# A hybrid decoder block on one core: another order of seven products, denser block sums, a later second norm, and factors stored in two parts

## The chip, the cores and the metric

One core of a Trainium2 chip runs the whole block as one program. The metric is the time on the device in microseconds, from three runs of the kernel before: 2037.86, 2042.06 and 2042.62, median 2042.06. Everything is float32 in memory. Every product is made of three matmuls on reduced-precision (fp32r) operands: each operand is split into a high part, rounded by a copy on ScalarE, and a low part, the difference, made by VectorE; the kernel adds high x high, high x low and low x high.

## What is computed

Sequence 512, width 2048, feed-forward width 8192, depth one. In the reference, cut to what matters here:

```
h  = rmsnorm(x, norm_mix_g);  z = h @ w_in           # (512, 2048) x (2048, 5128)
merged = [rmsnorm(attention(z)), rmsnorm(spatial_gating(z))]
x  = x + merged @ w_out                              # 2048 x 2048
h2 = rmsnorm(x, norm_ffn_g)                          # the second norm
a  = relu(h2 @ w_ff1)                                # the first product, 2048 x 8192
x  = x + (a * a) @ w_ff2                             # the second product, 8192 x 2048
out = rmsnorm(x, norm_final_g)
```

rmsnorm divides each row by the root of the mean of its squares (plus 1e-6) and multiplies by a gain. The root of the second norm is a number per token, so it commutes with the first product; a squared ReLU takes it as a square. The kernel therefore multiplies by it only at the very end, when the second product's sums are added to x (`settle`, with the square of the inverse root in `r2`).

## The kernel before

**The projections.** `run_units` goes over 224 steps: ten units of 16 steps for the input projection, then four units `oa` (attention half of the output projection) and four `og` (spatial-gating half) of 8 steps. A step loads and splits a piece of weights and issues 12 matmuls of 512 columns; pieces are split three steps ahead (`AHEAD`). After a step's matmuls `tick` runs the other tasks: each is a generator that yields the number of steps until its next turn.

**The handover.** When a unit `og` c ends, `g_done(c)` (L606) adds the two halves and x into `oa[c]`, squares them on ScalarE, adds the squares up over k on GpSimd (`ffn["ss"]`), starts the transposes of the result (`turn_x2`, stored in DRAM as `x2d`), scales by the gain (`scale_x2`) and makes the left operands of the first product (`make_forms`). For c = 3 the first product's loads and first three splits are issued first. `norm2_task` (L651) then sums over partitions with one-column matmuls and takes the root into `r2`.

**The products by Strassen and Winograd.** Both feed-forward products run as seven products of half-size blocks, P1 to P7, where eight would be usual; operands are sums of blocks (forms A11, A12, A22, S1 to S4 on the left; blocks b11, b12, b21, b22 and their sums on the right). In the first product 16 blocks u have 4 parts j of 7 products: 448 groups of 12 matmuls with 256 columns. `prepare` splits a group's weights three groups ahead. Two of the seven (P6 and P4) need a further block added into a tile that is already on the chip; before, this add stands directly ahead of the split. After part 3 each product's sum is taken out of its PSUM bank (`evacuate`), squared, and combined.

**The block sums.** `sums_task` (L679) makes b11 + b12 and b22 + b12 for all 64 pairs (u, j): three loads, two adds on VectorE, two stores to DRAM (`t1d`, `t3d`), from where `load` of the first product reads them two parts ahead. It starts at step 18 of the projections. Its buffers are one deep. Its instructions are marked to keep their place in the program's order.

**The factors.** After a block u, `factors_task` (L815) forms the seven left operands of the second product from the squares, splits each into a tile of 128 x 2 x 512 (high and low), from the pool `raw_pool` of four buffers, which the loads of w1 use too, and stores it in DRAM (`fac`).

**What sets the order.** TensorE's instructions run in the order of the program. Those of the other engines are put in order by a planner, when the program is built, from estimated durations, with the program's order as priority; at run time each engine keeps that order, and waits where an operand or a buffer is not ready. In the first product a tick comes after every second group, in the second product after every group.

## Time and profile before

| what | us |
|---|---|
| median of three runs | 2042.06 |
| the profiled execution | 2042.68 |
| its span, first to last instruction | 2040.1 |
| projections, up to the first matmul of the first product | 696.3 |
| first product (L806) | 696.3 to 1394.8 |
| second product (L1069) and the end | from 1394.8 |
| busy: TensorE, VectorE, ScalarE, GpSimd | 1988.1, 1600.3, 1040.3, 105.7 |

PE is TensorE, PEld its loading of weights, DVE VectorE, ACT ScalarE, POOL GpSimd, SP the engine that issues the DMAs. A row of a matmul lasts from issue to the modelled end, so rows overlap and their busy time is a union; the number of matmuls in a stretch says more than the busy time. In lists of groups and waits `fh` and `fl` are the high and low halves of w1, `form` the left operands, `q` the banks of the first product, `wh` and `wl` the halves of w2, `fc` the factors' staging tile, `b` the block sums' tiles, `t` the tiles that hold b11 and the sums in the first product.

### The profile page before, as it was taken

Reading aid. Unit: us, or ns where it says so; the run is one execution under the profiler, and the core shown is the slowest. Engines: PE = TensorE matmul, PEld = TensorE weight load, DVE = VectorE, ACT = ScalarE, POOL = GpSimd, SP = SyncE. Lnnn points to the kernel's source line nnn. Section 1 sums busy time; section 2 is a strip of 40 time slices with the busy share of each in tenths; the row PEclk is TensorE's granted clock in tenths of the full one; section 3 lists DMA queues with packets and bytes.
Section 4 is the critical chain, followed back from the end, with each engine's and each line's share of the span. In section 5 each row is a group of like instructions: output and inputs, shape, how many; then the busy total and the mean of one; then the engine's idle time right before and its main releaser. Section 6 shows DMA issues by size and latency. Waiting matters only on the chain.

```text
span 2040.1 us, 30501 instructions
## 1 busy us (share of the span) xinstructions
PE 1988.1 (97%) x11296; PEld 1733.7 (85%) x11296; DVE 1600.3 (78%) x2399; ACT 1040.3 (51%) x1676; POOL 105.7 (5%) x99
## 2 busy tenths in 40 slices
PE   9999999999999889999999999999999999999997
PEld 6888888888887789999999999998888888888875
DVE  7467467676658868888888788889888898898897
ACT  6344344455326555565565566666444444444455
POOL 5000001000222200000000000000000000000000
PEclk9999999999999989999999999999999999999999
DMA  6455554567555568888886665668836636646632
GB/s 222 136 168 165 170 165 156 188 199 263 181 186 181 181 217 276 288 289 302 296 279 220 224 223 202 217 233 332 333 128 240 246 130 237 240 137 234 244 137 83
DMA packets 209892, 435.69 MB, mean 214 GB/s; under 512 B 17744, under 2 KB 95696, under 8 KB 209616
## 3 DMA queue, kind: packets, MB, share of 16 engines
q1 hardware_dynamic: 209056, 431.89, 62.0%
q8 instruction: 88, 1.44, 0.3%
q10 hardware_dynamic: 432, 1.35, 0.2%
q0 software_dynamic: 256, 0.52, 0.2%
q14 instruction: 60, 0.49, 0.1%
HBM read 333.03 MB, written 100.66 MB: 213 GB/s over the span
## 4 chain that ended last, share of the span: by engine, by line
PE 39%; DVE 13%; DMA 6%; issue 3%; ACT 2%; SPq 1%; POOLq 0%; POOL 0%; ACTq 0%; DVEq 0%
PE bX L1069 16%; PE q L806 12%; PE bZ L1069 7%; DVE fl L744 4%; PE bY L1069 4%; DMA fac<-fc 3%; DMA b<-in_w_dram 2%; DVE fc L822 1%; DVE wl L902 1%; DMA r<-in_w_dram 1%; ACT fh L743 1%; DVE t L740 1%; DVE b L687 0%; DVE b L686 0%; DVE acc L950 0%
## 5 line engine op out<-in xcount | busy, mean ns | idle before, releaser
L806 PE MATMUL q<-form,fh 128*128 128x256 f32 x3584 | 657.8, 285 | 9.8 <-ACT fh L743 6.6
L806 PEld LDWEIGHTS q<-form,fh 128*128 128x128 f32 x3584 | 565.1, 193 | 13.3 <-ACT fh L743 9.3
L806 PE MATMUL q<-form,fl 128*128 128x256 f32 x1792 | 515.3, 288 | 17.5 <-DVE fl L744 16.9
L806 PEld LDWEIGHTS q<-form,fl 128*128 128x128 f32 x1792 | 346.5, 193 | 26.7 <-DVE fl L744 25.5
L901 ACT CAST wh<-raw 128x1024 fp32r<-128x1024 f32 x224 | 234.3, 1053 | 225.4 <-PE bX L1069 120.7
L902 DVE TENSOR_TENSOR wl<-raw,wh 128x1024 fp32r<-128x1024 f32 x224 | 271.1, 1223 | 72.5 <-ACT wh L901 71.7
L1069 PE MATMUL bX<-wh,fac 128*128 128x512 f32 x1008 | 320.9, 392 | 1.8 <-ACT wh L901 1.6
L743 ACT CAST fh<-t 128x512 fp32r<-128x512 f32 x256 | 155.0, 617 | 155.2 <-DVE t L738 67.6
L1069 PEld LDWEIGHTS bX<-wh,fac 128*128 128x128 f32 x1008 | 189.2, 188 | 49.5 <-ACT k_wh L922 6.4
L744 DVE TENSOR_TENSOR fl<-t,fh 128x512 fp32r<-128x512 f32 x256 | 173.9, 689 | 66.5 <-ACT fh L743 66.4
L1069 PE MATMUL bX<-wl,fac 128*128 128x512 f32 x504 | 198.3, 393 | 3.3 <-DVE wl L902 3.3
L1069 PE MATMUL bZ<-wh,fac 128*128 128x512 f32 x512 | 162.8, 389 | 0.0
L1069 PEld LDWEIGHTS bX<-wl,fac 128*128 128x128 f32 x504 | 94.6, 188 | 27.2 <-DVE wl L902 9.0
L1069 PEld LDWEIGHTS bZ<-wh,fac 128*128 128x128 f32 x512 | 96.1, 188 | 19.9
L150 PE MATMUL ps_qk<-xh,wh_qk 128*128 128x512 f32 x256 | 101.7, 397 | 0.0
L152 PE MATMUL ps_qk<-xh,wl_qk 128*128 128x512 f32 x256 | 100.0, 391 | 0.0
L151 PE MATMUL ps_qk<-xl,wh_qk 128*128 128x512 f32 x256 | 99.8, 390 | 0.0
L1069 PE MATMUL bZ<-wl,fac 128*128 128x512 f32 x256 | 99.6, 389 | 0.0
L744 DVE TENSOR_TENSOR fl<-r,fh 128x512 fp32r<-128x512 f32 x128 | 88.0, 687 | 10.5 <-ACT fh L743 10.5
L163 DVE SCALAR_TENSOR_TENSOR wl_qk<-raw_qk,cols,wh_qk 128x512 fp32r<-128x512 f32 x64 | 47.8, 750 | 61.2 <-ACT wh_qk L162 58.8
L162 ACT ACTIVATE wh_qk<-raw_qk,cols 128x512 fp32r<-128x512 f32 x64 | 46.3, 723 | 93.9 <-PE ps_qk L151 59.2
L743 ACT CAST fh<-r 128x512 fp32r<-128x512 f32 x128 | 79.0, 617 | 22.0 <-PE q L806 19.4
(621 smaller groups left out, 3594.8 us busy)
## 6 DMA issues: line engine op xcount, KB each, us to landing
b<-in_w_dram SPq DMA_DIRECT2D x256, 256.0 KB, 4.3
raw<-in_w_dram SPq DMA_DIRECT2D x128, 512.0 KB, 4.9
fac<-fc SPq DMA_DIRECT2D x112, 512.0 KB, 3.5
fac<-fac SPq DMA_DIRECT2D x112, 512.0 KB, 6.0
r<-in_w_dram SPq DMA_DIRECT2D x64, 512.0 KB, 5.1
raw_qk<-in_win_dram SPq DMA_DIRECT2D x32, 512.0 KB, 3.8
t1d<-b SPq DMA_DIRECT2D x64, 256.0 KB, 3.3
t3d<-b SPq DMA_DIRECT2D x64, 256.0 KB, 3.3
```

The costliest lines, as they stand in the source:

```text
L150: nc.tensor.matmul(ps, lhsT=ah, rhs=bh, start=start, stop=False)
L151: nc.tensor.matmul(ps, lhsT=ah, rhs=bl, start=False, stop=False)
L152: nc.tensor.matmul(ps, lhsT=al, rhs=bh, start=False, stop=stop)
L162: nc.scalar.activation(wh, raw, AF.Copy, scale=g)
L163: nc.vector.scalar_tensor_tensor(wl, raw, g, f(wh), ALU.mult, ALU.subtract)
L740: nc.vector.tensor_tensor(b[P4], b[P4], b[P2], ALU.add)
L743: nc.scalar.copy(pairs(wh), b[p])
L744: nc.vector.tensor_tensor(pairs(wl), b[p], pairs(f(wh)), ALU.subtract)
L806: nc.tensor.matmul(d, lhsT=l[:, c], rhs=r, start=j == 0 and q == 0 and m == 0 and w == 0, stop=j == 3 and q == 1 and w == 2, skip_group_ch ...
L901: nc.scalar.copy(wh, s)
L902: nc.vector.tensor_tensor(wl, s, f(wh), ALU.subtract)
L1069: nc.tensor.matmul(banks[chain][t], lhsT=l, rhs=r, start=start and w == 0, stop=stop and w == 2, skip_group_check=True)
```

## The change

Four edits. (1) The second norm's squares, their sum and the small matmuls leave the handover; in the second product a new task `second_norm` reads x back from DRAM in eight loads of 512 KB, squares it on ScalarE with a running sum over the row, and forms `r2`; it starts in the middle of the second product and takes a turn every three groups. (2) A block sum takes four steps instead of five. (3) The first product takes its seven products in the order P5, P1, P6, P2, P7, P4, P3; the adds for P6 and P4 are made right after the splits of P5 and P6; the forms at the handover follow the new order, and transposes of c = 2 use other PSUM banks. (4) The factors' high parts go two to a staging tile, the low parts are written over the form itself, and both are stored on their own.

```
-                if k == 0:
-                    ffn["ss"] = const.tile([P, 512], F32, tag="ssum", name="ssf")
-                    nc.scalar.activation(ffn["ss"], o, AF.Square)
-                else:
-                    nc.scalar.activation(t, o, AF.Square)
-                    nc.gpsimd.tensor_tensor(ffn["ss"], ffn["ss"], t, ALU.add)
...
             elif c == 2:
-                make_forms(c, (A11, A12))
+                make_forms(c, (S1, A11))
             else:
-                make_forms(2, (S1, S2, S3, S4, A22))
-                make_forms(3, (A11, A12, S1, S2, S3, S4, A22))
-            if c == 3:
-                start_task(norm2_task(), 6)
+                make_forms(2, (S2, A12, S3, A22, S4))
+                make_forms(3, (S1, A11, S2, A12, S3, A22, S4))
...
-            pt = mm(f"px{c}_{m}") if c == 3 else ax(f"px{c}_{m}", m % 2)
+            pt = mm(f"px{c}_{m}") if c > 1 else ax(f"px{c}_{m}", m % 2)
...
+    first = (P5, P1, P6, P2, P7, P4, P3)
...
                 here(nc.sync.dma_start(out=t3d[u][j], in_=b22))
-                yield 2
+                yield 1
...
         def prepare(i):
-            if p == P6:
-                nc.vector.tensor_tensor(b[P6], b[P6], b[P3], ALU.add)
-            if p == P4:
-                nc.vector.tensor_tensor(b[P4], b[P4], b[P2], ALU.add)
...
             nc.vector.tensor_tensor(pairs(wl), b[p], pairs(f(wh)), ALU.subtract)
             ready[i] = wh, wl
-            if p == P4:
+            if p == P5:
+                nc.vector.tensor_tensor(b[P6], b[P6], b[P3], ALU.add)
+            if p == P6:
+                nc.vector.tensor_tensor(b[P4], b[P4], b[P2], ALU.add)
+            if p == P3:
                 load(*divmod(4 * u + j + 2, 4))
...
-        def put(i):
-            t = raw_pool.tile([P, 2, 512], F32R, tag="raw", name=f"fc{u}_{i}")
-            nc.scalar.copy(t[:, 0, :], form[i])
-            nc.vector.tensor_tensor(t[:, 1, :], form[i], f(t[:, 0, :]), ALU.subtract)
-            nc.sync.dma_start(out=fac[u][i], in_=f(t).rearrange("p a c -> p (a c)"))
...
+        for i in range(0, NF, 2):
+            n = min(2, NF - i)
+            yield 2
+            t = raw_pool.tile([P, 2, 512], F32R, tag="raw", name=f"fc{u}_{i}")
+            for k in range(n):
+                nc.scalar.copy(t[:, k, :], form[i + k])
+                nc.vector.tensor_tensor(form[i + k].bitcast(F32R), form[i + k], f(t[:, k, :]), ALU.subtract)
+                nc.sync.dma_start(out=fac[u][i + k][:, 512:1024], in_=form[i + k])
+            nc.sync.dma_start(out=fac[u][i:i + n, :, 0:512].rearrange("i p c -> p i c"), in_=f(t)[:, 0:n, :])
...
+        def second_norm():
+            for th in range(2):
+                for q in range(4):
+                    x2 = load_x2(th, q)
+                    for t in range(2):
+                        tb = 2 * th + t
+                        nc.scalar.activation(x2[:, t, :], x2[:, t, :], AF.Square, accum_out=sums[:, tb, q:q + 1])
+                    yield 3
+            nc.vector.tensor_reduce(r2, sums, axis=AX.X, op=ALU.add)
+            inv_root(r2, r2, D, NT)
+            nc.vector.tensor_tensor(r2, r2, r2, ALU.mult)
...
+            if (kc, n, p, h) == (NK // 2, 0, P1, 0):
+                start_task(second_norm())
```

## Rows read from the trace of the kernel before

**Rows 1.** Of the page, busy us (share) xinstructions; clock in tenths, forty slices.

```profile
PE 1988.1 (97%) x11296; PEld 1733.7 (85%) x11296; DVE 1600.3 (78%) x2399; ACT 1040.3 (51%) x1676; POOL 105.7 (5%) x99
...
PEclk9999999999999989999999999999999999999999
```

**Rows 2.** Windows of L806: length, PE and PEld busy (xinstructions), clock, DMA, GB/s.

```profile
696.30:759.50 63.20, 48.20 (x336) 45.74 (x337) 0.86 0.54 168
759.50:890.60 131.10, 126.41 (x1011) 123.40 (x1010) 0.99 0.85 290
890.60:1107.20 216.60, 208.34 (x1682) 203.12 (x1681) 1.00 0.81 279
1107.20:1394.80 287.60, 285.50 (x2354) 283.03 (x2352) 1.00 0.65 228
```

**Rows 3.** The waits of TensorE over the span: us in total, times, longest.

```profile
PE q L806 <- DVE fl L744: 16.9, 32, 3.5
...
PE ps_og L152 <- DVE wl_og L163: 2.9, 2, 1.9
```

**Rows 4.** Windows, all engines: PE, PEld, DVE, ACT, POOL, clock, DMA, GB/s.

```profile
635.00:640.00 5.00, 3.42 (x8) 2.75 (x9) 3.51 (x6) 0.07 (x1) 0.00 (x0) 0.66 0.72 226
...
696.20:722.50 26.30, 15.09 (x80) 13.43 (x80) 25.31 (x36) 15.19 (x28) 5.91 (x4) 0.74 0.37 120
...
1500.00:1950.00 450.00, 450.00 (x1959) 365.00 (x1959) 399.11 (x423) 207.17 (x232) 0.00 (x0) 1.00 0.57 206
```

**Rows 5.** The source view of L686: ns min/median/max, first and last start.

```profile
L686 DVE TENSOR_TENSOR b<-b,b x64: 681/685/1793, 73.0 to 1063.9; 128x512 f32<-128x512 f32 x64
```

**Rows 6.** DMA issues: KB each, median us from issue to landing.

```profile
b<-in_w_dram SPq DMA_DIRECT2D x256, 256.0 KB, 4.3
...
fac<-fc SPq DMA_DIRECT2D x112, 512.0 KB, 3.5
...
t1d<-b SPq DMA_DIRECT2D x64, 256.0 KB, 3.3
...
x2l<-x2d SPq DMA_DIRECT2D x8, 512.0 KB, 6.0
```

**Rows 7.** The waits of all engines over the span, ScalarE's rows.

```profile
ACT fc L821 <- DMA fac<-fc: 63.7, 52, 3.9
...
ACT fh L743 <- DVE t L738: 67.6, 36, 4.4
...
ACT fh L743 <- DVE t L740: 42.5, 28, 4.1
```

**Rows 8.** Groups of instructions: busy us, mean ns of one, idle before and releaser.

```profile
L744 DVE TENSOR_TENSOR fl<-t,fh 128x512 fp32r<-128x512 f32 x256 | 173.9, 689 | 66.5 <-ACT fh L743 66.4
...
L743 ACT CAST fh<-t 128x512 fp32r<-128x512 f32 x256 | 155.0, 617 | 155.2 <-DVE t L738 67.6 <-PE q L806 42.9 <-DVE t L740 42.5
```

**Rows 9.** The timeline of GpSimd: start, us, engine, line, operation.

```profile
703.23 1.46 POOL L623 TENSOR_TENSOR ssf<-ssf,x 128x512 f32<-128x512 f32 x1 [1.42 <-ACT x L622]
...
731.19 1.02 POOL L123 TENSOR_TENSOR rt_ffn<-rt_ffn,neg_half 128x4 f32<-128x4 f32 x1 [20.72 <-DVE rt_ffn L122]
```

**Rows 10.** The timeline of VectorE at the handover.

```profile
702.88 0.68 DVE L738 TENSOR_TENSOR t<-t,r 128x512 f32<-128x512 f32 x1
...
703.48 1.76 DVE L617 TENSOR_TENSOR oa<-oa,x 128x512 f32<-128x512 f32 x1
...
709.25 1.77 DVE L686 TENSOR_TENSOR b<-b,b 128x512 f32<-128x512 f32 x1
```

**Rows 11.** The timeline of TensorE at the handover, idle before in brackets.

```profile
714.37 0.39 PE L806 MATMUL q<-form,fh 128*128 128x256 f32 x1 [2.40 <-ACT x2t L647]
...
718.30 0.58 PE L806 MATMUL q<-form,fl 128*128 128x256 f32 x1 [3.55 <-DVE fl L744]
...
729.88 1.02 PE L129 MATMUL pr_ffn<-one_col,ssf 128*128 128x1 f32 x8 [0.89 <-ACT x2t L647]
```

**Rows 12.** The source view of L952, ScalarE's square with a sum.

```profile
L952 ACT ACTIVATE x2l<-acc x16: 614/623/636, 1951.6 to 2025.6; 128x512 f32<-128x512 f32 x16
```

More of the change, by code (lines that the diff above doesn't have):

```diff
@@ L123, in inv_root, with sum_inv_root @@
         nc.gpsimd.tensor_tensor(dst, dst, neg_half[:, 0:1].broadcast_to([P, m]), ALU.pow)
-    def sum_inv_root(r, ss, n, name, bank=None):
-        pr = bank or ax(f"pr_{name}", 1)
+    def sum_inv_root(r, ss, n, name):
+        pr = ax(f"pr_{name}", 1)
         for tb in range(NT):
@@ L580, in hybrid_block @@
     oa = {}
-    ffn = {}
     part = {}
@@ L649, in turn_x2 @@
             yield 2
-    def norm2_task():
-        r = sm.tile([P, NT], F32, tag="rt", name="rt_ffn")
-        sum_inv_root(r, ffn["ss"], D, "ffn", mm("pr_ffn"))
-        nc.vector.tensor_tensor(r2, r, r, ALU.mult)
-        yield 1
     NF = 7
@@ L719, in first_product @@
     def first_product():
-        groups = [(u, j, p) for u in range(NU) for j in range(4) for p in usual]
+        groups = [(u, j, p) for u in range(NU) for j in range(4) for p in first]
         blocks, ready, banks = {}, {}, {}
@@ L756, in evacuate @@
             ps = banks[p]
-            if p == P1:
+            if p == P5:
                 sq["a"], sq["b"] = s8(f"sqa{u}_", F32, sx_pool), s8(f"sqb{u}_", F32, sx_pool)
@@ L778, in evacuate @@
                 square(b2)
+                start_task(factors_task(u, [a1, b2, b1, a0, a3, a2, b3], b0))
             else:
@@ L781, in evacuate @@
                 square(b0)
-                start_task(factors_task(u, [a1, b2, b1, a0, a3, a2, b3], b0))
         load(0, 0)
@@ L827, in factors_task @@
         nc.vector.tensor_tensor(s3, a11, a21, ALU.subtract)
-        for i in (A11, A12):
-            put(i)
-            yield 1
         nc.vector.tensor_tensor(s2, s1, a11, ALU.subtract)
         nc.vector.tensor_tensor(s4, a12, s2, ALU.add)
-        for i in (A22, S1, S3, S2, S4):
-            put(i)
-            yield 1
+        for i in range(0, NF, 2):
[7 more added lines that the diff above has]
+            nc.sync.dma_start(out=fac[u][i:i + n, :, 0:512].rearrange("i p c -> p i c"), in_=f(t)[:, 0:n, :])
     def second_product():
```

## The prediction

> **What bounds the kernel now.** I read the shares of the engines first. TensorE is busy 97% of the span and no other engine comes near [rows 1], so the time is TensorE's own work plus the stalls between its matmuls. The clock line shows full speed but for two dips [rows 1]. A matmul's row lasts two to three times as long as the distance to the next, so short stalls do not show as idle; I count matmuls per stretch instead. Each block u of the first product (28 groups of 12 matmuls) needs at best the pace of the last seven: 287.6 / 7 = 41.1 us [rows 2]. The first block took 63.2, the next three 131.1 / 3 = 43.7, the five after them 216.6 / 5 = 43.3 [rows 2]. Over the pace that is 22.1, 7.8 and 11.1 us, 41 in all, nearly everything that lies between 696 and 1395. The waits list says for whom: for VectorE's low halves of the weights (L744) above all [rows 3]. Before the first product there are two waits for VectorE, 2.9 us [rows 3], with the clock at 0.66 over five us after the first of them [rows 4], 0.34 x 5 = 1.7 us lost: 4.6 together. The second product runs without idle (450 of 450) while VectorE is at 399 and ScalarE at 207 [rows 4]; the change has nothing to win there. So what counts is what frees VectorE and ScalarE between 620 and 1107.
>
> **The block sums, one in four steps.** The last sum is made at 1063.9 [rows 5], at the border of the eighth and the ninth block (890.6 + 4 x 43.3 = 1063.8): the slow blocks are those with a sum among them, and the one that reads the last of them. The task starts at step 18. With 5 steps a sum, (224 - 18) / 5 = 41 of 64 are begun in the projections, and the other 23 take 114 steps of two groups, 228 groups, 8.1 blocks, which fits the row. With 4 steps, 51.5 are begun there and 50 steps are left: 100 groups, 3.6 blocks. Blocks five to nine then go at 41.1: -11.1 us. In the first four blocks, and in the projections, sums come more often by a quarter. A sum needs its store to land (3.3), the next load to land (4.3) [rows 6] and two adds (0.7 each [rows 5]): 9.0 us. The step of four gives 8 x 1.47 = 11.7 in the first product (1.47 is 41.1 / 28) and 4 x 2.76 = 11.0 in the projections (a step is 12 matmuls of 450 / 1959 = 0.23 us, by the count of matmuls of that shape in the second product [rows 4]). It fits, with 2 us to spare; what it adds I put at nothing, since weights are split three steps ahead and a late add delays only that lead. Ends: 0, and for a chain of 15.7 us (990.9 / 63, the mean distance of adds [rows 5]) the price in the rivals.
>
> **The other order of the seven products.** ScalarE waited 67.6 us for the add of L738 and 42.5 for that of L740 [rows 7]: both add into the tile that is split next, and stand directly in front of the split. In the new order each add is made right after an earlier split of the same tile, two or three groups ahead of its use, so add, high half and low half (0.69 + 0.62 + 0.69 [rows 8]) no longer stand in one chain in front of a group of 1.47 us. The same number of adds, splits and evacuations is left. In blocks two to four this works against the denser sums: a block of 28 groups holds 3.5 sums instead of 2.8, 0.7 x 1.4 = 1.0 us more for VectorE. I take -2.5 of the 7.8; ends -7.8 and +12 (a stall of one us for each of 12 sums).
>
> **The second norm's sums.** Sixteen squares on ScalarE, fifteen adds on GpSimd of 1.5 us [rows 9], a few one-column matmuls and their chain leave the handover. The adds cost more than their own engine: an add of VectorE from two tiles takes 0.68 alone and 1.76 to 1.77 beside GpSimd [rows 9, 10]. Between 696 and 722 VectorE is busy 25.3 of 26.3 [rows 4] and TensorE waits for it: three such adds (L617) and one sum (L686) are slow by 1.1 each, 4.4 us. TensorE's wait at 729.88 (0.89) and its one-column matmuls (1.02) go too [rows 11]: 1.9. The lower clock there (0.74 over 26.3 us [rows 4]) follows the idle of TensorE, and with 6 us less of that I take 1 more. Against it: the block now opens with P5, whose tile is loaded third of four; +0.5. In all -6.8; ends +2 (all cover lost: VectorE is bound by its 24 forms and adds in any case) and -14. The wait of 2.40 at 714.37 for a transposed copy [rows 11] also goes, as those banks are now others, but the 3.55 us for VectorE behind it stay; it is worth nothing. In the out-projection the same slowed adds push back the splits that TensorE waited for; of the 4.6 us I take -3.5, ends 0 and -4.6.
>
> The Trainium skill has a rule on this, in "SBUF — State Buffer", section "Who interferes with whom": a VectorE instruction with two inputs in SBUF and a GpSimd instruction that reads SBUF exclude each other for the whole instruction. By that rule the 1.1 us go wholly with the adds, as summed; were the slow rows owed to something that stays, the term would be -2.4 instead. By that rule the trace agrees: the slow rows begin while an add of GpSimd runs [rows 9, 10].
>
> What is added in the second product: eight loads of 512 KB, sixteen squares of 0.62 [rows 12], 10 us of an engine that is idle more than half of that stretch, and one power on GpSimd (1.02 [rows 9]) for which VectorE waits once. A square stands right behind its own load, which lands in 6.0 us [rows 6]; behind it on ScalarE are the high halves of w2, and VectorE waits for those. They are made two groups ahead, 5.5 us, of which 2 x (0.62 + 0.69) = 2.6 are work (the same two operations on twice the columns [rows 8]); some 2.9 us are cover. I take +2 in all. Ends 0 (the planner puts other work first) and 8 x (6.0 - 2.9) = 25.
>
> **The factors' low parts in place.** Each block's seven tiles of high and low become four of high parts; the work on VectorE and ScalarE is the same, and eleven stores go out, not seven. ScalarE waited 63.7 us for a staging tile's store [rows 7], over all blocks, the fast ones included, so that wait did not reach TensorE: 0. New is that the two tiles of squares are held until the last low part has landed. That part is issued at tick 10 of 14, group 17; the first square of the next block is written after group 21 and the second tile's after group 25. A store takes 3.5 us [rows 6], four groups are 5.9. Ends 0 and +0.7 a block (12 blocks, 8 us).
>
> The Trainium skill, "DMA: Bandwidth & Descriptors", section "Anatomy of one DMA — SWDGE (gpsimd) path", puts some 2 us fixed on each transfer, whatever its size. By it four stores more a block would add some 8 us of latency, an estimate, spread over queues; it speaks against the split, but would count only if a store ended last. That 256 KB land in 3.3 and 512 KB in 3.5 [rows 6] agrees.
>
> **Sum**, against the profiled execution (2042.7; span 2040.1 and 2.6 around it): -3.5 (out-projection) - 6.8 (first block) - 2.5 (blocks two to four) - 11.1 (five to nine) + 2 (second norm) = -21.9, so 2020.8. That execution lies 0.6 above the median of the runs, 2042.06, so the forecast is 2020.
>
> **Rivals.**
> (a) Everything opens: the whole 4.6, 14 of the first block, 7.8 and 11.1, and nothing for the norm: 2042.1 - 37.5 = 2005. For it: the stalls of blocks two to four sit at the two groups whose add moves away. Against: VectorE still has 24 operations at the handover. 0.15.
> (b) The handover and blocks two to four stay: only 11.1 and 3.5 come, less 2: 2029. For it: VectorE is full at 696 to 722 and the denser sums cost as much as the order gives. 0.17.
> (c) Slower: the sums' chain becomes the bound. Place: the first 3.6 blocks, where adds keep their place in VectorE's order and splits stand behind them. If a sum takes its measured 15.7 us also at step four, each of 12.5 sums delays TensorE by 15.7 - 11.7 = 4.0, 50 us, against 19.4 won elsewhere: 2042 + 31 = 2073. It decides from 11.7 + 19.4 / 12.5 = 13.3 us a sum. For it: a store's landing had to be awaited before the next load. Against: 9.0 by its parts. 0.07.
> (d) The squares hold ScalarE for their loads, 20 us more than I took, near that end: 2040. Against: ScalarE is mostly waiting for TensorE in that stretch. 0.08.
> (e) The change does not do what it says: the planner delays the adds or sums to where they were, and the rest cancels: 2042. 0.03.
> My forecast has 0.50, with 2011 to 2027 as its own range.
>
> **Numbers.** Below 0.3% (6 us) no change can be told from none with this kernel. Faster by more: the forecast, (a), (b): 0.82, and a little of (d): 0.83. Within: rest of (d), (e): 0.10. Slower: (c), 0.07. The range runs from just under (a) to past (b): 2003 to 2035; it leaves out (c), most of (d), (e) and a tail of (a).
>
> **What would show it.** Right: the last sum near 865; blocks from the fifth on at 41.1; no row of VectorE's two-tile adds at 1.7; the first block at 54 to 58; TensorE without idle in the second product while the eight loads are read. Wrong: blocks two to four over 46 with VectorE waiting for loads of b (c), stalls in the second product right behind those loads (d), a first block still over 60 (b), or ScalarE's first evacuation waiting for a low part's store (in place).

## The result, and the profile after

The changed kernel takes 2019.93 us (median of four runs, 2019.39 to 2020.05) against 2041.62 of the kernel before (four runs, 2037.86 to 2042.62): a ratio of 0.9897 [0.9879, 0.9914]. The forecast was 2020 (2003 to 2035). The profiled execution took 2020.05, its span is 2018.2.

The total came out as forecast; the parts did not. The table cuts both spans where a stage's first matmul starts. Each stage, here and below, is read from one profiled execution, while whole executions of the kernel before differ by up to 9.7 us (2034.57 to 2044.27), so a difference of a microsecond or two in one stage says little.

| stage, us | before | after | difference | forecast |
|---|---|---|---|---|
| input projection | 506.0 | 510.1 | +4.1 | 0 |
| output projection | 188.9 | 187.1 | -1.8 | -3.5 |
| wait before the first product | 1.4 | 8.8 | +7.4 | in the next |
| first block | 63.2 | 56.6 | -6.6 | -6.8 |
| blocks two to four | 131.0 | 122.8 | -8.2 | -2.5 |
| blocks five to nine | 216.7 | 201.6 | -15.1 | -11.1 |
| last seven blocks | 287.6 | 282.2 | -5.4 | 0 |
| second product and end | 645.2 | 649.0 | +3.8 | +2 |
| span | 2040.1 | 2018.2 | -21.9 | -21.9 |

The page of the kernel after, shares and clock, beside [rows 1]:

```profile
PE 1974.2 (98%) x11288; PEld 1729.7 (86%) x11288; DVE 1598.8 (79%) x2400; ACT 1052.4 (52%) x1692; POOL 84.4 (4%) x84
...
PEclk9999999999999989999999999999999999999998
```

VectorE does the same work as before and GpSimd's adds of squares are gone. But for the last slice here, both clock lines have one digit below 9, at the handover; I had read two dips in [rows 1]. The second, 0.66 at 635 to 640, shows only in [rows 4], and it is gone: the same five us have 1.00 now. Next the windows of the first product's matmuls (L791 here, L806 before), cut as in [rows 2]: length, PE and PEld busy, clock, DMA share, GB/s.

```profile
706.00:762.60 56.60, 46.86 (x337) 45.06 (x338) 0.86 0.65 204
762.60:885.40 122.80, 122.41 (x1011) 121.42 (x1010) 1.00 0.92 314
885.40:1087.00 201.60, 201.60 (x1683) 201.60 (x1682) 1.00 0.68 222
1087.00:1369.20 282.20, 282.20 (x2354) 282.16 (x2352) 1.00 0.70 232
```

From the second block on TensorE has nearly no idle: 0.39 us in three blocks where [rows 2] has 4.7 (131.1 - 126.4). The last seven, which I had taken as the best pace, went from 41.1 to 282.2 / 7 = 40.3 a block. The loss moved ahead of the first product. The waits of TensorE from 60 to 770 (us in total, times, longest), to hold against [rows 3]:

```profile
PE q L791 <- ACT fh L723: 8.4, 1, 8.4
PE q L791 <- DVE fl L724: 8.4, 2, 7.6
PE pS L150 <- DVE mx L382: 3.1, 4, 1.2
```

The third row is new: attention waits for a row maximum. One of its four cases, in the timeline of all engines (start, length, engine, line; in brackets the idle time before and what ended it):

```profile
174.15 1.23 DVE L670 TENSOR_TENSOR b<-b,b 128x512 f32<-128x512 f32 x1 [1.69 <-DMA b<-in_w_dram]
...
175.30 0.34 DVE L382 CUSTOM_DVE_ANT_0 p<-pS,nFm,mx 128x128 f32<-128x128 f32 x1
...
175.79 0.41 PE L150 MATMUL pS<-qkh 128*128 128x384 f32 x1 [0.92 <-DVE mx L382]
```

VectorE reaches the first add of a block sum (L670), finds its tile not landed, and stands 1.69 us; the maximum (L382) is the next in its order, and TensorE waits for that. The list of VectorE's waits between 60 and 700 has `DVE b L670 <- DMA b<-in_w_dram: 14.0, 9, 2.6` and 1.3 for the other add; before, this wait came to 0.7 for the adds. The first row of the list, 8.4, is the handover. SP's timeline there, and what ScalarE and TensorE made of it:

```profile
694.23 0.34 SPq L673 DMA_DIRECT2D t1d<-b  x1
695.92 0.34 SPq L674 DMA_DIRECT2D t3d<-b  x1
696.61 0.38 SPq L668 DMA_DIRECT2D b<-in_w_dram  x1
697.05 0.52 SPq L638 DMA_DIRECT2D x2d<-x2t  x1
697.68 1.15 SPq L668 DMA_DIRECT2D b<-in_w_dram  x2
698.88 0.49 SPq L712 DMA_DIRECT2D b<-in_w_dram  x1
699.47 0.41 SPq L714 DMA_DIRECT2D t<-t1d  x1
```

```profile
705.36 0.62 ACT L723 CAST fh<-t 128x512 fp32r<-128x512 f32 x1 [6.81 <-DMA t<-t1d]
```

```profile
706.03 0.58 PE L791 MATMUL q<-form,fh 128*128 128x256 f32 x1 [8.43 <-ACT fh L723]
```

SP takes its DMAs in order. The two stores of one sum and the three loads of the next one stand ahead of the load of `t1` (L714), which the first group now needs; it is issued at 699.47, 2.3 us after TensorE's last matmul of the projections (697.22), and ScalarE starts on it at 705.36, 5.9 us later. SP itself stood still on the way: its waits from 685 to 702 begin with `SPq L673 <- DVE b L670: 3.9, 2, 3.1`, the sum's store that waits for the late add. The granted clock is low in the wait and behind it. Windows with all engines (PE, PEld, DVE, ACT, POOL, clock), against [rows 4]:

```profile
697.00:706.00 9.00, 0.60 (x3) 0.18 (x1) 1.29 (x2) 1.78 (x4) 0.00 (x0) 0.73 0.90 279
706.00:723.00 17.00, 9.31 (x53) 8.61 (x53) 16.29 (x27) 10.71 (x19) 0.00 (x0) 0.70 0.17 52
...
1500.00:1950.00 450.00, 449.23 (x1952) 363.67 (x1951) 396.51 (x422) 210.41 (x241) 0.00 (x0) 1.00 0.58 208
```

The first add of a sum and VectorE's add at the handover, source views (ns min/median/max, first to last start), against [rows 5, 10]:

```profile
L670 DVE TENSOR_TENSOR b<-b,b x64: 667/686/1534, 73.1 to 864.3; 128x512 f32<-128x512 f32 x64
...
L615 DVE TENSOR_TENSOR oa<-oa,x x12: 681/687/692, 625.6 to 713.2; 128x512 f32<-128x512 f32 x12
```

The last sum is at 864.3, forecast near 865. No add of L615 is over 0.69 us any more. The sign that I had named, no two-tile add at 1.7, holds at the handover alone: one second add of a sum (L671) takes 1.78 at 535.96, while GpSimd adds x in the output projection (L601, 532.93 to 538.88). ScalarE's waits over the span, against [rows 7]:

```profile
ACT fh L723 <- DVE t L728: 13.3, 18, 1.9
...
ACT fc L814 <- DMA fac<-fc: 4.2, 6, 1.4
ACT fh L723 <- DVE t L730: 3.7, 3, 1.4
```

The two adds that stood ahead of a split cost ScalarE 17.0 us where they cost 110.1, and the staging tile 4.2 where it cost 63.7.

In the second product one stall is new, before the stretch 1500 to 1950 that I had priced. ScalarE and TensorE there:

```profile
1388.22 0.63 ACT L936 ACTIVATE x2l<-x2l 128x512 f32<-128x512 f32 x1
1388.76 0.19 ACT L936 ACTIVATION_READ_ACCUMULATOR x2l<-x2l 128x1 f32 x1
1388.85 0.62 ACT L936 ACTIVATE x2l<-x2l 128x512 f32<-128x512 f32 x1
...
1392.66 0.62 ACT L814 CAST fc<-sqb__15154 128x512 fp32r<-128x512 f32 x1
1393.18 0.62 ACT L814 CAST fc<-sqa__15153 128x512 fp32r<-128x512 f32 x1
1393.70 0.58 ACT L905 COPY k_wl<-bX 128x512 f32<-128x512 f32 x1
...
1394.34 0.80 PE L1067 MATMUL bX<-wh,fac 128*128 128x512 f32 x1 [2.10 <-ACT k_wl L905]
```

The program starts `second_norm` in the middle of the second product; the planner put its squares (L936) at 1388.2 to 1432.2, some 20 us into it, where the last block's factors (L814) and the first evacuations (L905) also want ScalarE. TensorE waits 2.1, and the granted clock from 1389 to 1399 is 0.83. The +3.8 is not this stall alone. Counted by matmuls, the first 2352 of the second product's 2688 take 542.9 us before and 544.6 after; the rest, in which both kernels do the same, takes 102.3 and 104.4.

### The profile page after: what moved, and what is told of

It is laid out like the page before. It is cut to its first block, busy times and chain, and to the rows that moved or that the text cites. A ratio compares the mean times of both kernels' runs of the same rounds, so it can differ in the third digit from the quotient of the medians.

```text
span 2018.2 us, 30643 instructions
## 1 busy us (share of the span) xinstructions
PE 1974.2 (98%) x11288; PEld 1729.7 (86%) x11288; DVE 1598.8 (79%) x2400; ACT 1052.4 (52%) x1692; POOL 84.4 (4%) x84
## 4 chain that ended last, share of the span: by engine, by line
PE 62%; DVE 3%; issue 1%; DMA 1%; ACT 1%; SPq 0%; POOLq 0%; POOL 0%; DVEq 0%; ACTq 0%
PE q L791 32%; PE bX L1067 16%; PE bZ L1067 8%; PE bY L1067 4%; DVE wl L885 1%; PE ps_og L152 1%; PE ps_og L150 1%; PE ps_og L151 1%; DVE acc L946 0%; DVE acc L913 0%; PE px L636 0%; PE pt L970 0%; DVE acc L914 0%; DMA t<-t1d 0%; DVE raw L878 0%
## 5 line engine op out<-in xcount | busy, mean ns | idle before, releaser
L791 PE MATMUL q<-form,fh 128*128 128x256 f32 x3584 | 650.9, 284 | 8.4 <-ACT fh L723 8.4
L791 PEld LDWEIGHTS q<-form,fh 128*128 128x128 f32 x3584 | 562.7, 193 | 8.8 <-ACT fh L723 8.8
L791 PE MATMUL q<-form,fl 128*128 128x256 f32 x1792 | 510.3, 285 | 8.9 <-DVE fl L724 8.7
L791 PEld LDWEIGHTS q<-form,fl 128*128 128x128 f32 x1792 | 345.9, 193 | 10.6 <-DVE fl L724 10.0
L150 PE MATMUL ps_qk<-xh,wh_qk 128*128 128x512 f32 x256 | 101.6, 397 | 0.0
```

Source lines behind the costliest of these rows:

```text
L150: nc.tensor.matmul(ps, lhsT=ah, rhs=bh, start=start, stop=False)
L791: nc.tensor.matmul(d, lhsT=l[:, c], rhs=r, start=j == 0 and q == 0 and m == 0 and w == 0, stop=j == 3 and q == 1 and w == 2, skip_group_ch ...
```

## The experiments

**A** is the prediction's account: the sums' earlier end frees blocks five to nine, denser sums cost nothing, the norm frees the handover, the order is a small gain. **B**, the rival: the order frees all blocks, and the denser sums cost time in the projections and at the handover. The first four kernels tell them apart.

**Block sums alone** (kernel before, a sum in four steps).

```diff
                 here(nc.sync.dma_start(out=t3d[u][j], in_=b22))
-                yield 2
+                yield 1
```

> The kernel before with one edit: a block sum every four steps. Theory A (the prediction's): the blocks of the first product are slow because sums stand among them, and denser sums cost the projections nothing: first matmul of the first product at 696, blocks two to four at 43 to 44, five to nine at 41.1, total about 2030. Theory B (from the trace of after): the first product's stalls come from the adds in front of the splits, and denser sums hold up the projections: first product begins 5 to 8 us later, blocks two to four at 44 to 46, five to nine at 41 to 42, total 2035 to 2042.

Measured: 2049.11 against 2040.72, 1.0038 [1.0025, 1.0051], slower. Windows with all engines over blocks two to four and five to nine, and VectorE's wait (60 to 700), which was 0.7 before:

```profile
770.00:904.40 134.40, 126.69 (x1010) 123.43 (x1009) 111.71 (x181) 76.03 (x136) 0.00 (x0) 0.99 0.86 292
904.40:1109.70 205.30, 204.09 (x1683) 202.23 (x1682) 168.29 (x271) 127.22 (x226) 0.00 (x0) 1.00 0.64 218
```

```profile
DVE b L686 <- DMA b<-in_w_dram: 8.7, 7, 1.7
```

A's mechanism is there: 205.3 instead of 216.7, -11.4, my -11.1. But blocks two to four lose 3.4, the projections 4.2 and 2.4, the wait before the product 3.5, and in all it is slower: what I had put at nothing is larger than the gain. The direction is B's; the total lies above both ranges, and the first product begins 10.1 us later, not 5 to 8.

**The order alone** (kernel before with the new order of products, its forms and banks, and the early adds, which now stand behind the split).

```diff
+    first = (P5, P1, P6, P2, P7, P4, P3)
...
-            if p == P6:
-                nc.vector.tensor_tensor(b[P6], b[P6], b[P3], ALU.add)
-            if p == P4:
-                nc.vector.tensor_tensor(b[P4], b[P4], b[P2], ALU.add)
...
             ready[i] = wh, wl
...
+            if p == P5:
+                nc.vector.tensor_tensor(b[P6], b[P6], b[P3], ALU.add)
+            if p == P6:
+                nc.vector.tensor_tensor(b[P4], b[P4], b[P2], ALU.add)
```

> The kernel before with one edit: the order of the seven products with the early adds, the forms' order and the other banks of the transposes. Sums stay at five steps, so they reach into the ninth block. Theory A: only part of the stalls of blocks two to four goes, five to nine stay near 43.3: total 2035 to 2041. Theory B: the stalls go although sums are still made beside them: blocks two to nine at 40.3 to 41, the last seven at 40.3, total 2015 to 2022, with up to 8 us lost at the handover where the first group waits for the load of its sum.

Measured: 2024.10, 0.9914 [0.9897, 0.9931]. Windows as above, blocks two to four, five to nine, the last seven:

```profile
759.00:883.80 124.80, 122.88 (x1010) 121.45 (x1009) 110.77 (x179) 78.24 (x136) 0.00 (x0) 1.00 0.86 295
883.80:1091.70 207.90, 204.22 (x1683) 202.31 (x1682) 182.59 (x295) 129.51 (x226) 0.00 (x0) 1.00 0.86 295
1091.70:1374.80 283.10, 282.77 (x2355) 282.36 (x2354) 238.40 (x378) 182.54 (x314) 0.00 (x0) 1.00 0.68 231
```

-6.2, -8.8 and -4.5, with the sums running on to the ninth block (VectorE has 295 instructions in blocks five to nine, 271 where they had ended). One edit, which I had given 2.5, is worth 16.6 us. That is nearest to B, but B had more: blocks two to nine take 41.6, not 40.3 to 41, and the total is 2 us above its range. The second product is 4.6 longer (649.8) though this kernel has no second norm in it: 544.3 in its first 2352 matmuls, 105.5 in the rest.

**The second norm alone** (the squares and `norm2_task` taken out of the handover, `second_norm` put in).

```diff
-                    nc.scalar.activation(t, o, AF.Square)
-                    nc.gpsimd.tensor_tensor(ffn["ss"], ffn["ss"], t, ALU.add)
...
-                start_task(norm2_task(), 6)
...
+                        nc.scalar.activation(x2[:, t, :], x2[:, t, :], AF.Square, accum_out=sums[:, tb, q:q + 1])
...
+                start_task(second_norm())
```

> The kernel before with one edit: the second norm's squares and sums in the second product. Theory A: output projection 3 to 4.6 us shorter, first block 5 to 7 shorter, second product up to 2 longer: total 2031 to 2035. Theory B: the same two gains at the front, but the planner makes the squares at the very start of the second product, beside the last block's factors: 3 to 5 us more there, total 2034 to 2038.

Measured: 2029.64, 0.9939 [0.9924, 0.9954]. The output projection takes 185.4 (-3.5, as forecast), the first block 57.4 (-5.8), the second product 646.4 (+1.2; 542.3 in its first 2352 matmuls, so the squares, at 1406.9 to 1473.2 and some 25 us into it, cost nothing there). VectorE's adds at the handover, timeline:

```profile
695.91 0.69 DVE L617 TENSOR_TENSOR oa<-oa,x 128x512 f32<-128x512 f32 x1
...
709.91 0.69 DVE L678 TENSOR_TENSOR b<-b,b 128x512 f32<-128x512 f32 x1
```

Both kinds took 1.76 and 1.77 beside GpSimd [rows 10]. The Trainium skill, "SBUF — State Buffer", section "Who interferes with whom", has a VectorE instruction with two inputs in SBUF and a GpSimd instruction that reads SBUF exclude each other; by that rule VectorE's adds run at their own 0.69 once GpSimd's have left, and this trace agrees. A holds for this edit; the total is 1.4 us better than its range, and blocks two to four are 2.8 shorter, which neither theory had.

**After, a sum in five steps again.**

```diff
                 here(nc.sync.dma_start(out=t3d[u][j], in_=b22))
-                yield 1
+                yield 2
```

> The kernel after with the block sums back at five steps. Theory A: the sums reach into the ninth block again and with them the stalls of blocks five to nine, 11 us: total 2026 to 2031. Theory B: blocks two to nine stay within 1 us of 40.3, the projections win back 5 to 6 us and the first group's wait for its sum (8.8 us) shrinks to 1 to 4: total 2006 to 2013.

Measured: 2006.92, 0.9831 [0.9815, 0.9847], 13.0 under the kernel after. Input projection 506.5, output projection 185.5, wait 2.7, first block 54.1; blocks five to nine, with a sum in most of them:

```profile
871.10:1074.60 203.50, 203.14 (x1682) 202.01 (x1682) 181.94 (x295) 129.96 (x226) 0.00 (x0) 1.00 0.89 300
```

203.5 against 201.6: with the new order, ending the sums early is worth 1.9 us, and it costs 3.6 + 1.6 + 6.1 + 2.5 before. SP's timeline shows why the wait is gone: the load of `t1` is issued at 690.84, not 699.47.

```profile
690.84 0.62 SPq L714 DMA_DIRECT2D t<-t1d  x1
```

**The factors alone** (kernel before with the new `factors_task` body).

```diff
-            t = raw_pool.tile([P, 2, 512], F32R, tag="raw", name=f"fc{u}_{i}")
-            nc.scalar.copy(t[:, 0, :], form[i])
-            nc.vector.tensor_tensor(t[:, 1, :], form[i], f(t[:, 0, :]), ALU.subtract)
...
+                nc.scalar.copy(t[:, k, :], form[i + k])
...
+                nc.vector.tensor_tensor(form[i + k].bitcast(F32R), form[i + k], f(t[:, k, :]), ALU.subtract)
+                nc.sync.dma_start(out=fac[u][i + k][:, 512:1024], in_=form[i + k])
```

> The kernel before with one edit: the factors' low parts in place, high parts two to a tile. Theory A (the prediction's): no effect, within 2 us of before, first product's blocks as before. Theory B: the staging tiles' waits on ScalarE held up the high halves too, so blocks two to nine gain 1 to 2 us each and the last seven go from 41.0 to 40.3 or so: total 2028 to 2034.

Measured: 2045.90 against 2040.50, 1.0031 [1.0021, 1.0042] over ten runs, slower. The last seven blocks:

```profile
1102.60:1398.00 295.40, 288.06 (x2354) 283.84 (x2353) 239.54 (x380) 179.48 (x314) 0.00 (x0) 1.00 0.66 222
```

42.2 a block instead of 41.1, though ScalarE's wait for the staging tile's store (60 to 1398) fell to 9.5. In a block the extra time is 0.62 and 1.08 at two groups, where copies now come in pairs ahead of a split that also waits for its add; that this is the cause is argued, not tested. The whole loss is in these seven blocks (+7.8); blocks two to nine gain 4.9. So my zero fails, and B's gain too.

**After with five steps, but the old factors.**

```diff
-        for i in range(0, NF, 2):
-            n = min(2, NF - i)
-            yield 2
...
+        for i in (A22, S1, S3, S2, S4):
+            put(i)
+            yield 1
```

> The kernel after with sums at five steps and with the factors stored as before (high and low in one tile, one store each). If the factors edit gives nothing: 2005 to 2009 as with it, blocks at 40.3 to 41. If it was what took the stalls out of the blocks: blocks two to sixteen at 41 to 42.4 and total 2014 to 2025. The stall of 2.5 us some 23 us into the second product goes if the last block's factors caused it, and stays if the second norm's squares did.

Measured: 2015.17, 0.9869 [0.9852, 0.9885]. The same edit that costs 5.4 alone is worth 8.3 here (2015.17 - 2006.92): -1.6 in blocks two to four, -5.4 in blocks five to nine. ScalarE's wait for staging stores (60 to 1369) is 40.6 here and 5.2 with the edit. That wait reaches TensorE only in blocks that hold sums: in blocks two to nine it is 26.6 here and TensorE waits 4.8 for the low halves (0.5 with the edit); in the last seven it is 14.0, TensorE waits nowhere, and they take 282.3 (283.0 with the edit). The stall of 2.5 at the start of the second product is gone, as expected if the last block's factors caused it; distances of 1.64 and 1.38 between two matmuls stand near its place, and the second product, 648.4, is not shorter.

**After with five steps, the second norm kept where the program puts it.**

```diff
-            nc.sync.dma_start(out=t, in_=x2d[q][:, 2 * th:2 * th + 2, :])
+            keep(nc.sync.dma_start(out=t, in_=x2d[q][:, 2 * th:2 * th + 2, :]))
...
-                    x2 = load_x2(th, q)
+                    x2 = load_x2(th, q, here)
+                    yield 2
...
-                        nc.scalar.activation(x2[:, t, :], x2[:, t, :], AF.Square, accum_out=sums[:, tb, q:q + 1])
-                    yield 3
+                        here(nc.scalar.activation(x2[:, t, :], x2[:, t, :], AF.Square, accum_out=sums[:, tb, q:q + 1]))
+                    yield 1
```

> The kernel after with sums at five steps and with the second norm's loads and squares kept at their place in the program, in the middle of the second product, squares two groups behind their load. If the planner's moving them to the start costs: the stall of 2.5 us some 23 us into the second product goes, second product 645 to 646 instead of 647.2, total 2004.5 to 2006. If ScalarE waits for their loads in the new place (rival d of the prediction): 2 us or more longer there, stalls of TensorE right behind the eight loads, total 2009 to 2015.

Measured: 2010.70, 0.9849 [0.9834, 0.9863], 3.8 more. The stall at the start of the second product shrinks from 2.51 to 1.90 and two small ones come in the new place (0.65 at 1731, 0.22 at 1754):

```profile
1729.54 0.64 ACT L937 ACTIVATE x2l<-x2l 128x512 f32<-128x512 f32 x1 [0.61 <-DMA x2l<-x2d]
...
1731.39 0.50 PE L1068 MATMUL bX<-wh,fac 128*128 128x512 f32 x1 [0.65 <-ACT k_wh L905]
```

That is my rival (d) in small: a square holds ScalarE for its load and TensorE pays. But it does not account for the 3.8. The first 2352 matmuls of the second product take 544.0, against 544.9 with five steps: the start wins more than the new place costs (1.3). The two profiled spans are 2006.8 and 2004.9, and the wait before the first product and the first block, where the code is the same, are 1.2 us longer each. The squares are not the whole cause of the stall at the start.

**After, a sum in six steps.**

```diff
                 here(nc.sync.dma_start(out=t3d[u][j], in_=b22))
-                yield 1
+                yield 3
```

> The kernel after with a block sum every six steps, so that sums reach into block thirteen. If every step of density costs: input projection at 506, out-projection and the wait at the handover each 0.5 to 1.5 us shorter than with five, blocks at 40.3 to 41 to the thirteenth: total 2002 to 2006. If sums in the first product still cost 0.5 us a block: four more blocks, 2 us, total 2007 to 2010. If a sum comes too late for its load: blocks past the tenth at 43 and more.

Measured: 2011.67, 0.9856 [0.9839, 0.9874]: 4.8 above five steps and outside all that I had expected. VectorE waits for `b` only 1.9 us (60 to 700), but one stall of 3.3 us stands at 326 to 330 in attention (`PE pS L150 <- DVE mx L382: 3.3, 1, 3.3`), and the second product has the 2.51.

The next two ask whether a sum's number of steps decides (its density), or the wait between its loads and its adds.

**Four steps, three of them between loads and adds.**

```diff
-                yield 2
+                yield 3
                 here(nc.vector.tensor_tensor(b11, b11, b12, ALU.add))
                 here(nc.vector.tensor_tensor(b22, b22, b12, ALU.add))
-                yield 1
```

> The kernel after, still one sum in four steps, but with three steps instead of two between a sum's loads and its adds, and the stores right behind the adds. If the projections lose time because VectorE stands at an add whose load has not landed (and attention's maxima stand behind it): VectorE's waits for loads of b go from 15 us to under 3, input projection 506 to 507.5 instead of 510.1, the first group's wait at the handover under 5 instead of 8.8, total 2009 to 2014. If it is the extra work and traffic by themselves: input projection stays at 509 to 511, total 2017 to 2021.

Measured: 2017.01, 0.9886 [0.9864, 0.9908], 2.9 under after. VectorE's waits for `b` (60 to 700) are `DVE b L671 <- DMA b<-in_w_dram: 5.0, 4, 2.2` and 1.9 for the other add, 6.9 in all, not 15.3, and the handover's wait is 4.7, not 8.8; but the input projection stays at 509.9: the four small stalls gave way to one of 2.63 that ends at 329. A later add is not enough.

**Five steps, three of them between loads and adds** (as above, and two steps behind the stores).

```diff
                 here(nc.sync.dma_start(out=t3d[u][j], in_=b22))
-                yield 1
+                yield 2
```

> One sum in five steps with the same three steps of lead. If at five steps the loads already land in time: no change to five steps as they were, 2005 to 2009, input projection 506. If the late loads still cost at the handover: its wait of 2.7 us goes to under 2 and the first block shortens by 1 to 2, total 2003 to 2006.

Measured: 2017.12, 0.9889 [0.9871, 0.9908]. Five steps, and nearly as slow as after, outside both ranges: 510.3 in the input projection, 8.7 at the handover. Density falls as the cause. The stall at 326, GpSimd, VectorE and TensorE:

```profile
323.66 0.29 POOL L475 TENSOR_SCALAR_AFFINE_SELECT ws<-ws 128x128 f32<-128x128 f32 x1 [4.34 <-DMA ws<-in_ws_dram]
...
328.26 0.80 DVE L478 TENSOR_TENSOR wsl<-ws,wsh 128x128 fp32r<-128x128 f32 x1 [1.98 <-ACT wsh L477]
328.98 0.34 DVE L382 CUSTOM_DVE_ANT_0 p<-pS,nFm,mx 128x128 f32<-128x128 f32 x1
...
329.48 0.41 PE L150 MATMUL pS<-qkh 128*128 128x384 f32 x1 [3.10 <-DVE mx L382]
```

No add of a block sum is in it. A piece of the spatial weights (L478), for whose load GpSimd waits, stands in front of the maximum. It stands there with five steps and in the kernel before too, but there its load lands in time. With five steps:

```profile
321.98 0.29 POOL L475 TENSOR_SCALAR_AFFINE_SELECT ws<-ws 128x128 f32<-128x128 f32 x1 [1.62 <-DMA ws<-in_ws_dram]
...
326.11 0.80 DVE L478 TENSOR_TENSOR wsl<-ws,wsh 128x128 fp32r<-128x128 f32 x1 [0.31 <-ACT wsh L477]
```

What differs is the traffic beside the load of 64 KB: here SP issues a sum's two stores and the next one's three loads at 317.65 to 322.65, and the DMA share is 1.00 from 319 to 325; with five steps they come at 325.02 to 328.16, and it is 0.52. With six steps and in the kernel above SP issues them in the same place (from 318.68 and 317.76) and one of the two loads makes GpSimd wait 3.72 and 4.49. So a sum's transfers hold up attention here by delaying another load; that the traffic is the reason is read from the times, no run separates it.

**Five steps, the load of `t1` first of the four.**

```diff
-            b11, t1, t3 = (pairs(t2(f"{n}_{u}{j}")) for n in ("b11", "t1", "t3"))
+            t1, b11, t3 = (pairs(t2(f"{n}_{u}{j}")) for n in ("t1", "b11", "t3"))
...
+            nc.sync.dma_start(out=t1, in_=pairs(t1d[u][j]))
...
-            nc.sync.dma_start(out=t1, in_=pairs(t1d[u][j]))
```

> One sum in five steps, and the first product's load issues the sum t1, which the first group needs, ahead of b11 and r. If the place of that load in the queue of four is what delays the first group: wait at the handover 1.4 to 2 instead of 2.7, total 2005 to 2006.5. If the queue stands before all four (for a buffer or a store of the sums): unchanged, 2006 to 2008.

Measured: 2008.04, 0.9843 [0.9824, 0.9862]: the wait before the first product falls from 2.7 to 1.4, and the whole is the same as five steps (2006.92) within what can be told; the first block took 55.2 instead of 54.1.

**Four steps, begun one step earlier.** If place and not number decides, moving the whole train of sums by one step must be enough.

```diff
-    start_task(sums_task(), 18)
+    start_task(sums_task(), 17)
```

> The kernel after, one sum in four steps, with the sums begun one step earlier (17, not 18). In the order of the DMA queue one sum's stores and the next one's loads less then stand ahead of the first product's first loads. If it is the place of the sums in the order that costs: the first group's wait at the handover goes from 8.8 to 1.4 to 4 us and the input projection changes by more than 1 us in either direction, total 2008 to 2015. If it is their number alone: wait 7 to 9, input projection 509 to 511, total 2017 to 2021.

Measured: 2008.39, 0.9847 [0.9830, 0.9865], 11.5 under after, by one character. Input projection 507.0, output projection 185.8, wait 2.6, first block 54.1. VectorE's waits for `b` (60 to 700) and SP's timeline at the handover:

```profile
DVE b L670 <- DMA b<-in_w_dram: 7.9, 3, 3.3
```

```profile
691.65 0.63 SPq L714 DMA_DIRECT2D t<-t1d  x1
...
694.30 0.42 SPq L673 DMA_DIRECT2D t1d<-b  x1
...
695.25 5.25 SPq L668 DMA_DIRECT2D b<-in_w_dram  x3
```

The stores and loads of the next sum now stand behind the product's loads. VectorE waits 8.9 us for `b` in all, but at places where little stands behind: TensorE's own wait for a maximum is 0.6 once. So the sums cost the kernel after its 11.5 by where they fall, not by how many there are in a stretch. This kernel and the two with five steps and the old lead (2006.92, 2008.04) are the fastest; they can't be told apart.

## Why the prediction was right in its total, and where its steps failed

The total was right by luck: errors of both signs met, +4.1 (input projection), +7.6 (handover and first block, +0.8 instead of -6.8), +1.7 (output projection) and +1.8 (second product) against -5.7, -4.0 and -5.4 in the blocks. What held: the second norm's move, the order and the sums' end each shorten the stage that I had named. Step by step:

- **The block sums, "what it adds I put at nothing": failed, by some 11 us.** I compared a sum's length with its period, and it fits on average. An add keeps its place in VectorE's order, so each late landing holds what stands behind it, and that is not the split three steps ahead but, in attention, a maximum for which TensorE waits at once; at 326 it is another load, which lands late beside a sum's transfers. I had named who is behind only for splits. Rival (c) had the mechanism, but at the wrong place (the first blocks) and at 50 us. Its 15.7 us a sum was a misreading: that is the distance of two sums at five steps, not a sum's length; at four steps the distance is 791.2 / 63 = 12.6 us, from the first and last start of L670.
- **The handover, "whose tile is loaded third of four; +0.5": failed, it was +7.4.** What counted was not the order among four loads (moving `t1` to the front is worth 1.3 in the wait and nothing in total) but what SP had to issue ahead of them. I did not walk through SP's queue, past the sum's stores. The first block goes with its granted clock, but the clock does not go with the wait: 56.6 us at 0.86 in the kernel after and 54.1 at 0.91 with five steps (wait 2.7), but 57.7 at 0.85 with six steps and a wait of 2.8, and 55.2 at 0.90 with five steps, three of lead and a wait of 8.7.
- **Blocks five to nine: -15.1 for -11.1, but not for my reason alone.** The sums' end gives 11.4 by itself with the old order; the order gives 8.8 by itself; with the order, the sums' end adds 1.9. Both cure the same stalls, so the two don't add. In [rows 2] a slow block and a block with a sum were the same blocks, and I read that as cause; the experiment shows that the add in front of the split was the other half.
- **The order, -2.5 in blocks two to four: mis-sized; by itself -6.2 there and -16.6 in all.** The two waits of ScalarE that I quoted, 67.6 and 42.5 [rows 7], fall to 11.2 and 6.5 with the order alone. I had given it nothing in the other blocks; alone it shortens all of them.
- **"Needs at best the pace of the last seven, 41.1": failed.** The pace without stalls is 40.3. [Rows 2] showed most of it: the loading of weights is busy 283.03 of 287.60, 4.6 us short, where 5.4 went. The pace was taken from a stretch that had the very waits.
- **The second norm: right.** Alone -5.8 in the first block and -3.5 in the output projection, forecast -6.8 (the order's part in it included) and -3.5. In the kernel after, the output projection gives only -1.8, since the sums' place costs 1.3 to 1.6 of it: the other versions with the norm moved have 185.4 to 185.8, but for the one of four steps with three of lead (187.2).
- **The squares, +2 in the second product: no such cost is shown.** The second product is +3.8 in the kernel after, but +1.2 with the norm alone and +4.6 with the order alone, which has no squares there. Of the 3.8 some 1.7 lie in the first 2352 matmuls, where the planner drew the squares to the start and the stall of 2.1 stands; 2.1 lie in the rest, whose code did not change. In the middle, where I had put the cost, TensorE has 449.23 of 450; with the squares kept there it is 1.3. The distance of matmuls at the stall is 2.5 in several versions and 1.9 without squares, with the old factors the stall is gone, and the version with the norm alone has no new one: several edits crowd ScalarE there. Which one ends it is open.
- **The factors at nothing: failed twice.** +5.4 alone, -8.3 with the other three edits at five steps. That the wait of 63.7 "did not reach TensorE" I took from its standing in the fast blocks as well, but the fast blocks were not free of stalls. With the order changed and the old factors, TensorE loses time beside that wait in the blocks that hold sums and none in the last seven. Why the edit alone lengthens the last seven is argued above, not shown. In ScalarE's waits of the first product, down to 0.2 us, no evacuation has a low part's store behind it, so the part on the held tiles was right. No run prices the 2 us a store that the prediction quotes from the Trainium skill; the title of that section names GpSimd's path, and these stores are issued by SP.

Alone, the four edits come to +8.4 (sums), -16.6 (order), -11.1 (norm) and +5.4 (factors), -13.9 in all; together they made -21.7. So the edits don't add. Two changes of price are measured: the factors' from +5.4 to -8.3, and the sums' from +8.4 to +13.0 (the kernel after against the one with five steps). No run splits the rest.

Open: the stall at the start of the second product, the loss of the factors' edit alone, and what sets the granted clock in the first block.

## What to carry to other kernels

When a stream of loads, adds and stores is woven into a queue by count of steps, don't ask only whether it fits its period: walk through each in-order queue that it passes (SP's too) and see what stands behind its late element at the two or three tight places, and which other load is in flight beside its transfers; shifting its phase by one step may be worth more than its rate. The price of an edit holds for the kernel in which it was measured: the factors' edit cost 5.4 us in one and won 8.3 in another; measure such edits together as well as alone. The pace of the calmest stretch is a bound only if that stretch itself has no idle.

## What the runs showed of the hardware that was not expected

A square of ScalarE with its running sum is two rows: 0.63 us for the activation and 0.19 for the read of the accumulator behind it (628 and 188 ns median, 16 times). The rows overlap: in the lines above one square starts at 1388.22, its read at 1388.76 and the next square at 1388.85. So a square with its sum takes 0.63 us of ScalarE and sixteen take 10, as forecast, not the 13 that the rows add up to; two casts of the same size, with rows of 0.62, start 0.52 apart (1392.66 and 1393.18).

A small load can land much later beside larger ones. GpSimd's 64 KB load of `ws` kept it waiting 1.62 us at a DMA share of 0.56 (five steps, 319 to 322) and 4.34 at 1.04 (three steps of lead, the same stretch), and attention's maximum stood behind it. That the traffic is the reason is argued, not tested.

A long wait of TensorE need not lower the clock behind it. Over the 17 us behind the wait at the handover the granted clock was 0.70 after 8.4 us of idle time (the kernel after) and 0.77 after 2.3 (five steps), but also 0.70 after 2.4 (six steps) and 0.80 after 8.3 (five steps, three of lead).
